# A decoder trunk's feed-forward: the pool of the V sums opened first, and two additions queued behind a reciprocal

## The chip, the cores and the metric

The kernel runs on one core of a Trainium2 chip. The metric is the device time of one execution in microseconds (us). A profile of one further execution gives a span, from its first to its last instruction, and what each engine did in it. TensorE (PE) multiplies, with its weight loads listed apart (PEld); VectorE is DVE, ScalarE is ACT, GpSimd is POOL, and SP is the engine that issues most of the transfers.

## The reference

Two residual layers on 512 tokens of 1024 features, in float32, then one more norm. Each layer adds a mixer's output and then a SwiGLU feed-forward's, each computed from the normed stream:

```
for i in range(2):
    x = x + mixer_i(rmsnorm(x, norm_mix[i]))          # 0: causal pooling, 1: dilated window attention
    h = rmsnorm(x, norm_ffn[i])
    x = x + (silu(h @ w_gate) * (h @ w_up)) @ w_down   # 2816 hidden features
return rmsnorm(x, norm_final)
```

## The kernel before

Every float32 product is made of three matmuls. A tile is split into a rounded part `hi` (a copy on ScalarE, line 137 for weights and 312 for activations) and the rest `lo` (a subtraction on VectorE, lines 138 and 313), and TensorE sums `hi*hi`, `hi*lo` and `lo*hi`.

The feed-forward works on blocks of a 2 by 2 scheme with seven products in place of eight (a Winograd form). Gate and up weights of 128 columns are cut into blocks; for the group `n`, the products 0 to 6 (`Group.product`, line 601 holds its matmuls) use a block or a sum of blocks as weights, and on the right the normed tokens: first or last 256 tokens, first or last four chunks of features, or sums of these (`t2`, `t3`, `t4`, and `T_hi[0]`, the tokens' own place rewritten). The weights of products 1, 2 and 5 are sums. They are built in a tile `vraw`, one for each group: SP loads one block (line 104), GpSimd adds a second with an accumulating transfer (line 106), and VectorE adds and subtracts other raw tiles later (line 140). `vraw` tiles come from the pool `ffv`, three of 4 KB (`V_TILES`); all other raw weights come from a ring of five `wraw`, and their splits from a ring of five pairs `whi` and `wlo`. A raw tile that a sum still needs keeps its place in the ring until line 140 has run.

One list, `queue`, holds all weight tiles in the order of their use. `weights(i)` (line 119) issues loads some places ahead and splits four places ahead; `load_sums` (line 109) issues the `vraw` loads, and does so only once the pool of the feed-forward is open. TensorE's order is the one written in the code. The order of all other engines and of the DMA queues is set by a planner that takes, at each point of its own model, the instruction that is ready and has the best priority; those within `high_priority(URGENT)` come first. [...]

Memory is handed out as a stack: each pool lies behind the pools still open, in the order of opening. With `reuse_waits="tile"` an instruction that first writes a tile waits for the last readers of the tiles that lay there. At the start of a feed-forward the pools of the mixer before it are closed, so the feed-forward's pools begin at the same address as that mixer's. In the first layer there lie, from that address on, `p_hi` (16 KB a partition), `p_lo` (16 KB), the eight tiles `bhi` and `blo` of the pool `poolb` (the second half of the output weights, 32 KB) and one of 4 KB. In the second layer there lie `pT` (41 KB), `v` (16 KB) and some small tiles with `LB`, in one pool `attn`, then the pool `merged` (8 KB), then `wob`, the eight tiles `bhi` and `blo` there. In the feed-forward (`ffn`, line 514) the pools come in the order `ffn` (`t2` to `t4`, `keep`, `ct`, 34.25 KB), `ffv` (12 KB), `ffa` (28 KB) and `ffh` (`t1r`, `t2r`, `t3r`, `b21r` and `ct_second`, 24 KB).

The join of mixer and feed-forward is `out_projection` (line 342). It makes the last product of the mixer in two halves of columns. In the second half, block by block of 128 tokens, TensorE makes the product, VectorE adds it to the stream (line 340), ScalarE squares it (line 275), and `Norm.prepare` (line 297) makes the root: `inverse_rms` (line 286) is a square root on ScalarE (line 290) and four short VectorE steps on one column (lines 291 to 294), the last of which is the reciprocal by which ScalarE then scales the rows (line 303). The rows of blocks 0 and 1 are turned (transposed on TensorE, line 309) while the next products run, those of block 2 behind the last product, and those of block 3 within the feed-forward's first stage.

That stage is "two": two groups at once, in the order `TWO`, products 0 and 3 of both first since these need only blocks 0 and 1 of the tokens. Beside them the operands of the others are made. `first_tokens` (line 639) adds `hi` and `lo` of the first 256 tokens back into whole numbers, on VectorE (line 641): `t1r` from the first four chunks of features, `b21r` from the last four. `late(b, what)` (line 645) takes blocks 2 and 3 from TensorE's bank and makes `t1r`, `t2r`, `t3r` and their splits: `t1r` in line 651, read by the last step also from `b21r` in line 662. The first addition is written ahead of the stage's loop, the second at its fifth place:

```
first_tokens(0, t1r)
for at, (g, i) in enumerate(TWO):
    ...
    if at == 4:
        first_tokens(1, b21r)
```

After "two" come groups of seven products ("quad") and the down projections.

Of the kernel before, what the change touches and what calls it, by code (L numbers as in the profile page):

```python
# [57 lines left out]
def trunk_kernel(ctx: ExitStack, tc: tile.TileContext, x_in, xT, gam, gains, consts, ident_d, w0, wT, w1, wv, w_down, out):  # L58
# [9 lines left out]
    nc = tc.nc  # L68
# [17 lines left out]
    pools = {}  # L86
    RING = 5
    V_TILES = 3
# [150 lines left out]
    def tokens_at(shift):  # L239
        return [h[:, shift : shift + NC * S].rearrange("p (c s) -> p c s", c=NC) for h in h_both]  # L240
# [17 lines left out]
    class Norm:  # L258
# [27 lines left out]
        def inverse_rms(self, b):  # L286

            v, s, r = (tmp.tile([P, 1], F32, name=name, bufs=2) for name in ("v1", "s1", "r1"))
            first, second = self.ss[:, b, 0:1], self.ss[:, b, 1:2]
            nc.scalar.activation(s, second, AF.Sqrt, bias=first)  # L290
            nc.vector.tensor_add(v, first, second)
            nc.vector.reciprocal(r, s)
            nc.vector.tensor_scalar(v, v, r, s, op0=ALU.mult, op1=ALU.add)
            nc.vector.reciprocal(r, v)
            return r

        def prepare(self, b, parts=(slice(0, D),)):
# [89 lines left out]
    with ExitStack() as pctx:  # L387
        open_pool = lambda name, bufs, **kw: pctx.enter_context(tc.tile_pool(name=name, bufs=bufs, reuse_waits="tile", **kw))
# [37 lines left out]
        norm = Norm(None, spare)  # L426
# [11 lines left out]
        v, s, r = (tmp.tile([P, 4], F32, name=name) for name in ("v4", "s4", "r4"))  # L438
# [66 lines left out]
        norm = Norm(0, px.tile([P, D], F32, name="even_rows"))  # L505
# [8 lines left out]
    def ffn(layer, norm, third, nxt):  # L514
# [8 lines left out]
        with ExitStack() as fctx:  # L523
            open_pool = lambda name, bufs, **kw: fctx.enter_context(
                tc.tile_pool(name=f"{name}{layer}", bufs=bufs, reuse_waits="tile", **kw)
            )
            fp = open_pool("ffn", 1)
            fps = open_pool("ffps", 2, space=bass.MemoryType.PSUM)
            pools["v"] = open_pool("ffv", V_TILES)
            early_u = open_pool("ffa", 2)  # L530
            h_hi, h_lo = tokens_at(SHIFT)
            block = lambda t, k, n: t[:, 4 * k : 4 * k + 4, HALVES[n]]

# [103 lines left out]
            t1r, t2r, t3r, b21r = (hn.tile([P, 4, 256], F32, name=name) for name in ("t1r", "t2r", "t3r", "b21r"))  # L637

            def first_tokens(k, to):

                nc.vector.tensor_add(to, block(h_hi, k, 0).bitcast(F32), block(h_lo, k, 0).bitcast(F32))
# [3 lines left out]
            def late(b, what):  # L645
                js = slice((b - 2) * P, (b - 1) * P)
                tps = late_banks[b]
                at = lambda t: t[:, :, js]
                parts = lambda i: (at(T_hi[i]), at(T_lo[i]))
                if what == 1:  # L650
                    nc.vector.tensor_sub(at(t1r), at(t1r), tps[0])
                    split(*parts(0), at(t1r))
                    nc.scalar.copy(at(t3r), tps[0])
                elif what == 2:
                    nc.vector.scalar_tensor_tensor(at(t2r), at(t1r), -1.0, tps[1], op0=ALU.mult, op1=ALU.subtract)
                    split(*parts(1), at(t2r))
                elif what == 3:
                    nc.vector.tensor_sub(at(t3r), tps[1], at(t3r))
                    split(*parts(2), at(t3r))
                else:  # L660
                    split(at(block(h_hi, 1, 1)), at(block(h_lo, 1, 1)), tps[1])
                    nc.vector.scalar_tensor_tensor(at(t2r), at(t2r), -1.0, at(b21r), op0=ALU.mult, op1=ALU.subtract)
                    split(*parts(3), at(t2r))
# [4 lines left out]
            def down(b):  # L668

                pairs = BLOCKS[b]  # L670

                p, r = ([fps.tile([P, 2, 256], F32, name=t).rearrange("p g c -> p (g c)") for _ in range(2)] for t in "rp")
                q = [mm.tile([P, S], F32, name="mm") for _ in range(2)]
                where = (0, 1, 2, 3, 6, 5, 4)
                target = ((0, 0, 1), (1, 1, -1), (0, 1, 1), (0, 0, 1), (1, 1, -1), (0, 1, 1), (1, 0, -1))
                for i, acc in enumerate((p, r, p, q, p, r, p)):
                    ws = [weights(js[i], held=z) for z, js in enumerate(dn[b])]
                    half, n, sign = target[i]
                    for t in range(2):
                        for c, pair in enumerate(pairs):  # L680
                            whi, wlo = (w[:, c % 2, :] for w in ws[c // 2])
                            hi, lo = (u[:, where[i], t * P : (t + 1) * P] for u in u_of[pair])
                            for k, (u, w) in enumerate(((hi, whi), (hi, wlo), (lo, whi))):
                                nc.tensor.matmul(  # L684
                                    acc[t], lhsT=u, rhs=w, start=i in (0, 1, 3) and c + k == 0,
                                    stop=c == len(pairs) - 1 and k == 2, skip_group_check=True,
                                )
                        to = x[:, 2 * n + t, COLS[half]]
                        with tc.high_priority(URGENT):
                            if sign > 0:  # L690
                                nc.vector.tensor_add(to, acc[t], to)
                            else:
                                nc.vector.tensor_sub(to, to, acc[t])

            for kind, n in FFN_ORDER[:-1]:
                if kind == "two":
                    groups = [Group(n, ct_common), Group(n + 1, ct_tile(hn, "ct_second"))]
                    first_tokens(0, t1r)
                    for at, (g, i) in enumerate(TWO):
                        if at in (0, 2):  # L700
                            b = 2 + at // 2
                            if b == 2:
                                late_banks[b] = third
                                norm.prepare(3, COLS)
                            else:
                                late_banks[b] = [r_tile(), by_four(mm.tile([P, S], F32, name="mm"))]
                                for half in range(2):
                                    norm.turn(b, half, late_banks[b][half])
                            late(b, 1)
                        if at == 4:  # L710
                            first_tokens(1, b21r)
                        if at in (4, 6, 8):
                            for b in (2, 3):
                                late(b, at // 2)
                        groups[g].product(i)
                    held.close()
                    late_u.append(open_pool("ffb", 2))
                elif kind == "quad":
                    group = Group(n, ct_common)
                    for i in range(7):  # L720
                        group.product(i)
                else:
                    down(n)


            norm = Norm(nxt, ct_common.rearrange("p m n g c -> p (m n g c)")[:, :D])
# [58 lines left out]
        return norm  # L785

    norm = ffn(0, norm, third, 1)


    with ExitStack() as actx:  # L790
# [6 lines left out]
        at = 8 * SPAN  # L797
# [4 lines left out]
        v = ap.tile([P, 4, D], F32, name="v")  # L802
# [159 lines left out]
        for t in range(8):  # L962
# [6 lines left out]
            at = 2 * t + 3  # L969
# [92 lines left out]
        for part in range(2):  # L1062
            at = VA + part * VB
# [53 lines left out]
        norm = Norm(2, mp.tile([P, D], F32, name="even_rows"))  # L1117
# [3 lines left out]
        third = out_projection(j_wo, range(NC), m_hi, m_lo, norm, SHIFT, four, lambda: [sc_tile(), sc_tile()])  # L1121

    ffn(1, norm, third, 3)


# [65 lines left out]
```

## Time and profile before

| | us |
|---|---|
| median of 3 runs | 1018.32 (1017.35 to 1019.07) |
| the profiled execution's own time | 1018.40 |
| its span | 1016.6 |
| TensorE busy in the span | 1000.0 |
| VectorE busy | 792.8 |
| ScalarE busy | 530.0 |
| GpSimd busy | 121.0 |
| mean granted TensorE clock | 0.994 of full speed |

Times in the profile count from the start of the span. A line of a timeline gives the start, the duration, the engine, the line of the code, the operation and the names of what it writes and reads; in brackets stands how long the engine had been idle before it, and the instruction or transfer that ended this. Matmuls overlap in the pipeline: one is listed with 0.28 us though the next starts 0.12 us later. So the distance between starts tells the pace, and a matmul slowed by a lower clock counts as busy all the same. `SPq` lines are issues of transfers, not their duration.

### The profile page before, as it was taken

The numbers are of one execution on the slowest core, as the hardware profiler recorded it, in microseconds if no ns is written. First come the engines' busy times: TensorE is split into PE (matmuls) and PEld (weight loads), VectorE is DVE, ScalarE is ACT, GpSimd is POOL, SyncE is SP. The second block draws the span as 40 slices with busy tenths as digits, with TensorE's granted clock in tenths as the row PEclk, the third lists the DMA queues.
The fourth block names the chain that finished last, engine by engine and source line by source line (L and its number), as shares of the span: only waits on it lengthen the run. The fifth ranks groups of instructions, "written<-read, shape, count | busy, mean of one in ns | idle before, by whom it ended". The sixth has DMA issues, their size and how long they took to land.

```text
span 1016.6 us, 16615 instructions
## 1 busy us (share of the span) xinstructions
PE 1000.0 (98%) x6582; PEld 912.5 (90%) x6582; DVE 792.8 (78%) x1134; ACT 530.0 (52%) x836; POOL 121.0 (12%) x108
## 2 busy tenths in 40 slices
PE   9999989999999999999999999999999999999997
PEld 7888879989998998989777899889998999999895
DVE  6483689898888788777988747569989888888875
ACT  5572467545654554463344444357654564455454
POOL 0000101101011100001333210100101001111000
PEclk9999989999999999999999999999999999999999
DMA  9451467759559854514311246525866955975522
GB/s 346 157 186 21 117 194 193 175 170 260 142 129 248 222 142 139 183 57 145 103 42 52 75 124 175 116 63 160 203 150 192 237 149 118 287 187 138 154 71 83
DMA packets 76349, 155.16 MB, mean 153 GB/s; under 512 B 6448, under 2 KB 6576, under 8 KB 76272
## 3 DMA queue, kind: packets, MB, share of 16 engines
q1 hardware_dynamic: 58944, 121.00, 35.5%
q0 software_dynamic: 17040, 32.84, 19.1%
q8 instruction: 51, 0.84, 0.3%
q10 hardware_dynamic: 288, 0.27, 0.1%
q14 instruction: 26, 0.21, 0.1%
HBM read 151.99 MB, written 2.10 MB: 152 GB/s over the span
## 4 chain that ended last, share of the span: by engine, by line
PE 92%; DVE 3%; DMA 2%; ACT 2%; issue 1%; POOL 0%; SPq 0%; ACTq 0%; POOLq 0%
PE p L601 24%; PE r L601 13%; PE r L684 10%; PE mm L601 6%; PE p L684 5%; PE mm L222 4%; PE mm L224 3%; PE mm L223 3%; PE mm L738 3%; PE mm L684 2%; PE mm L354 2%; PE mm L352 2%; PE mm L353 2%; DMA vraw<-w 1%; PE mm L1073 1%; PE mm L1072 1%
## 5 line engine op out<-in xcount | busy, mean ns | idle before, releaser
L138 DVE TENSOR_TENSOR wlo<-wraw,whi 128x1024 fp32r<-128x1024 f32 (+2 forms) x190 | 220.4, 1161 | 76.6 <-ACT whi L137 76.0
L137 ACT CAST whi<-wraw 128x1024 fp32r<-128x1024 f32 (+2 forms) x190 | 185.2, 978 | 173.0 <-issue 34.7
L137 ACT CAST whi<-vraw 128x1024 fp32r<-128x1024 f32 (+1 forms) x102 | 99.4, 976 | 148.0 <-DVE vraw L140 51.6
L601 PE MATMUL p<-t_hi,wlo 128*128 128x256 f32 x528 | 149.9, 284 | 0.0
L601 PE MATMUL p<-t_lo,whi 128*128 128x256 f32 x528 | 149.9, 284 | 0.0
L601 PE MATMUL p<-t_hi,whi 128*128 128x256 f32 x528 | 148.7, 282 | 0.9 <-ACT ct L616 0.9
L138 DVE TENSOR_TENSOR wlo<-vraw,whi 128x1024 fp32r<-128x1024 f32 (+1 forms) x102 | 114.9, 1127 | 19.8 <-ACT whi L137 19.3
L601 PE MATMUL r<-h_hi,whi 128*128 128x256 f32 x352 | 100.3, 285 | 3.9 <-ACT h_hi L312 3.9
L601 PE MATMUL r<-h_lo,whi 128*128 128x256 f32 x352 | 101.1, 287 | 0.1
L601 PEld LDWEIGHTS p<-t_hi,whi 128*128 128x128 f32 x528 | 100.1, 189 | 1.1 <-ACT ct L616 1.1
L601 PE MATMUL r<-h_hi,wlo 128*128 128x256 f32 x352 | 101.0, 287 | 0.0
L601 PEld LDWEIGHTS p<-t_hi,wlo 128*128 128x128 f32 x528 | 99.8, 189 | 0.0
L601 PEld LDWEIGHTS p<-t_lo,whi 128*128 128x128 f32 x528 | 99.3, 188 | 0.1
L106 POOL DMA_DIRECT2D wraw<-w x22 | 26.8, 1216 | 429.3 <-DMA wraw<-w 93.2
L140 DVE TENSOR_TENSOR vraw<-vraw,wraw 128x1024 f32<-128x1024 f32 x68 | 76.6, 1127 | 0.8
L601 PEld LDWEIGHTS r<-h_hi,whi 128*128 128x128 f32 x352 | 67.9, 193 | 4.1 <-ACT h_hi L312 4.1
L601 PEld LDWEIGHTS r<-h_lo,whi 128*128 128x128 f32 x352 | 67.4, 191 | 0.4 <-DVE h_lo L313 0.4
L601 PEld LDWEIGHTS r<-h_hi,wlo 128*128 128x128 f32 x352 | 67.6, 192 | 0.0
L222 PE MATMUL mm<-h_hi,whi 128*128 128x512 f32 (+1 forms) x176 | 65.3, 371 | 0.0
L224 PE MATMUL mm<-h_hi,wlo 128*128 128x512 f32 (+1 forms) x176 | 63.6, 361 | 0.0
L223 PE MATMUL mm<-h_lo,whi 128*128 128x512 f32 (+1 forms) x176 | 63.5, 361 | 0.0
L684 PE MATMUL r<-wlo,u_hi 128*128 128x512 f32 x144 | 56.1, 390 | 0.0
(313 smaller groups left out, 2516.4 us busy)
## 6 DMA issues: line engine op xcount, KB each, us to landing
wraw<-w SPq DMA_DIRECT2D x116, 512.0 KB, 4.9
wraw<-w_down SPq DMA_DIRECT2D x32, 512.0 KB, 3.7
wraw<-w POOLq DMA_DIRECT2D x22, 512.0 KB, 7.5
vraw<-w SPq DMA_DIRECT2D x22, 512.0 KB, 5.0
vraw<-w POOLq DMA_DIRECT2D x22, 512.0 KB, 8.9
wraw<-wT SPq DMA_DIRECT2D x16, 512.0 KB, 3.8
wraw<-w_down SPq DMA_DIRECT2D x24, 256.0 KB, 2.7
vraw<-w_down SPq DMA_DIRECT2D x6, 512.0 KB, 5.4
```

The source lines that it names most:

```text
L106: nc.gpsimd.dma_start(dst, more, accum_op=ALU.add)
L137: nc.scalar.copy(hi[:, :n], raw[:, :n])
L138: nc.vector.tensor_sub(lo[:, :n], raw[:, :n], hi[:, :n].bitcast(F32))
L140: nc.vector.tensor_add(raws[into][:, :n], raws[into][:, :n], raws[more][:, :n])
L222: nc.tensor.matmul(ps, lhsT=whi, rhs=xhi, start=first, stop=False, **kw)
L223: nc.tensor.matmul(ps, lhsT=whi, rhs=xlo, start=False, stop=False, **kw)
L224: nc.tensor.matmul(ps, lhsT=wlo, rhs=xhi, start=False, stop=last, **kw)
L352: nc.tensor.matmul(ps, lhsT=xhi, rhs=w[0][:, k, :], start=first, stop=False)
L353: nc.tensor.matmul(ps, lhsT=xhi, rhs=w[1][:, k, :], start=False, stop=False)
L601: nc.tensor.matmul(ps[:, g, :], lhsT=w[:, g, c, :], rhs=xx[:, c, :], start=i in (0, 1, 3) and g + c + k == 0, stop=c == 3 and k == 2, skip ...
L684: nc.tensor.matmul(acc[t], lhsT=u, rhs=w, start=i in (0, 1, 3) and c + k == 0, stop=c == len(pairs) - 1 and k == 2, skip_group_check=True,)
L738: nc.tensor.matmul(ps, lhsT=u, rhs=w[:, m, :], start=z + m + k == 0, stop=z == 1 and m == 1 and k == 2,)
```

## The change

Three things. The pool of the `vraw` tiles is opened ahead of the feed-forward's other pools, so that its 12 KB come first in the memory and `t2` to `ct` follow behind them; the later pools stay where they were. `inverse_rms` keeps its last instruction, the reciprocal. And both additions of `first_tokens` are written ahead of the stage's loop, with an edge that puts them behind the reciprocal kept last, that of the third block, in VectorE's order (an order of issue; they don't wait for its end). Both feed-forwards run this code.

```
@@ inverse_rms
-            nc.vector.reciprocal(r, v)
+            self.chain = nc.vector.reciprocal(r, v)
@@ ffn
+            pools["v"] = open_pool("ffv", V_TILES)
             fp = open_pool("ffn", 1)
             fps = open_pool("ffps", 2, space=bass.MemoryType.PSUM)
-            pools["v"] = open_pool("ffv", V_TILES)
             early_u = open_pool("ffa", 2)
+            third_chain = norm.chain.ins
@@ ffn, the stage "two"
-                    first_tokens(0, t1r)
+                    with tc.issue_after(third_chain):
+                        first_tokens(0, t1r)
+                        first_tokens(1, b21r)
                     for at, (g, i) in enumerate(TWO):
...
-                        if at == 4:
-                            first_tokens(1, b21r)
```

## Rows read from the trace of the kernel before

**Rows 1.** The page's first part: busy time of each engine, its share of the span and its count of instructions.

```profile
PE 1000.0 (98%) x6582; PEld 912.5 (90%) x6582; DVE 792.8 (78%) x1134; ACT 530.0 (52%) x836; POOL 121.0 (12%) x108
```

**Rows 2.** TensorE's list of waits from 105 to 170 us: what waited, for what, then total time, times and the longest, in us.

```profile
PE r L601 <- ACT h_hi L312: 3.9, 1, 3.9
PE p L601 <- ACT ct L616: 0.9, 1, 0.9
PE mm L309 <- ACT even_rows L303: 0.7, 1, 0.7
```

**Rows 3.** TensorE's timeline around the join and the "two" stage of the first feed-forward: the last matmul of the out-projection, the first product, the first `r` product, and the first `r` product of the next quad.

```profile
113.55 0.39 PE L354 MATMUL mm<-bhi,h_lo 128*128 128x512 f32 x1
...
115.46 0.36 PE L601 MATMUL p<-h_hi,whi 128*128 128x256 f32 x1
...
131.89 0.58 PE L601 MATMUL r<-h_hi,whi 128*128 128x256 f32 x1 [3.86 <-ACT h_hi L312]
...
167.72 0.28 PE L601 MATMUL r<-h_hi,whi 128*128 128x256 f32 x1
```

**Rows 4.** TensorE's timeline at the same places of the second feed-forward (last matmul of the out-projection, first product, first `r` product of the next quad).

```profile
678.44 0.40 PE L354 MATMUL mm<-bhi,h_lo 128*128 128x512 f32 x1
...
679.46 0.37 PE L601 MATMUL p<-h_hi,whi 128*128 128x256 f32 x1
...
723.18 0.28 PE L601 MATMUL r<-h_hi,whi 128*128 128x256 f32 x1
```

**Rows 5.** The table by stretches: the stretch, its length, then busy time and count of PE, PEld, DVE, ACT and POOL, the granted clock, the share of the DMA engines and GB/s. The first line is the stage "two" of the first feed-forward, the second that of the second, then two pieces of the first.

```profile
115.46:167.72 52.26, 47.31 (x371) 46.46 (x370) 42.19 (x60) 31.25 (x46) 8.48 (x7) 0.93 0.84 220
679.46:723.18 43.72, 43.72 (x372) 43.72 (x371) 42.96 (x62) 31.44 (x47) 3.61 (x3) 1.00 0.61 169
134.00:138.00 4.00, 4.00 (x22) 4.00 (x21) 4.00 (x5) 1.82 (x2) 1.21 (x1) 0.53 0.12 39
146.00:147.50 1.50, 0.56 (x5) 0.35 (x3) 0.78 (x3) 1.50 (x4) 0.00 (x0) 1.00 0.68 225
```

**Rows 6.** Issues of transfers, from the timelines of SP and GpSimd: first feed-forward (SP, then GpSimd), then SP in the second.

```profile
63.48 8.07 SPq L104 DMA_DIRECT2D wraw<-w  x5
113.97 1.39 SPq L104 DMA_DIRECT2D vraw<-w  x3
...
77.00 1.34 POOL L106 DMA_DIRECT2D wraw<-w  x1 [76.55 <-DVE h_lo L488]
118.04 1.21 POOL L106 DMA_DIRECT2D vraw<-w  x1 [39.71 <-DMA vraw<-w]
...
633.31 1.59 SPq L104 DMA_DIRECT2D vraw<-w  x3
```

**Rows 7.** The timelines of ScalarE and VectorE in the stage "two" of the first feed-forward: the split of the first V tile, and what VectorE does behind it.

```profile
127.23 1.05 ACT L137 CAST whi<-vraw 128x1024 fp32r<-128x1024 f32 x1 [6.20 <-DMA vraw<-w]
...
128.32 1.23 DVE L138 TENSOR_TENSOR wlo<-vraw,whi 128x1024 fp32r<-128x1024 f32 x1 [5.96 <-ACT whi L137]
129.46 0.68 DVE L651 TENSOR_TENSOR t1r<-t1r,r 128x512 f32<-128x512 f32 x1
```

**Rows 8.** Last readers: of `p_hi` (TensorE, first layer), of `pT` and `v` (TensorE, second layer), of `LB` (VectorE, second layer).

```profile
73.66 0.39 PE L224 MATMUL early<-p_hi,wlo 128*128 128x512 f32 x1
...
629.72 3.55 PE L1099 MATMUL mm<-pT,v 128*64 128x128 f32 x51
...
637.95 1.06 DVE L1115 TENSOR_TENSOR o<-mm,LB 128x512 f32<-128x512 f32 x1
```

**Rows 9.** From the view of all instructions on `vraw`: the time from issue to landing of its transfers.

```profile
DMA to landing us min/median/max: 3.2/6.0/12.3
```

**Rows 10.** The first V tile in the second feed-forward, from the timelines of ScalarE and VectorE.

```profile
655.35 1.04 ACT L137 CAST whi<-vraw 128x1024 fp32r<-128x1024 f32 x1
...
658.36 1.22 DVE L140 TENSOR_TENSOR vraw<-vraw,wraw 128x1024 f32<-128x1024 f32 x1
```

**Rows 11.** Timelines of VectorE and ScalarE in the first layer: the first update of `x` and the first square in the second half of the out-projection, and the copy into `keep`.

```profile
95.85 0.69 DVE L340 TENSOR_TENSOR x<-mm,x 128x512 f32<-128x512 f32 x1 [3.15 <-PE mm L354]
...
96.58 0.63 ACT L275 ACTIVATE even_rows<-x 128x512 f32<-128x512 f32 x1 [4.66 <-DVE x L340]
...
119.95 0.57 ACT L612 COPY keep<-p 128x512 f32<-128x512 f32 x1
```

**Rows 12.** VectorE's timeline around the third block's root in the first layer.

```profile
110.78 1.20 DVE L641 TENSOR_TENSOR t1r<-h_hi,h_lo 128x1024 f32<-128x1024 f32 x1
111.91 0.27 DVE L293 TENSOR_SCALAR v<-v,r,s 128x1 f32<-128x1 f32 x1
...
113.22 0.15 DVE L294 RECIPROCAL r<-v 128x1 f32<-128x1 f32 x1
113.98 0.69 DVE L340 TENSOR_TENSOR x<-mm,x 128x512 f32<-128x512 f32 x1 [0.60 <-PE mm L354]
```

**Rows 13.** VectorE's timeline around the fourth block in the second layer.

```profile
678.87 0.69 DVE L340 TENSOR_TENSOR x<-mm,x 128x512 f32<-128x512 f32 x1 [2.61 <-PE mm L354]
...
683.26 0.16 DVE L294 RECIPROCAL r<-v 128x1 f32<-128x1 f32 x1
```

**Rows 14.** Groups of the page by line, engine and operands: count, busy us and mean ns of one, and the idle time before them.

```profile
L601 PE MATMUL p<-t_hi,whi 128*128 128x256 f32 x528 | 148.7, 282 | 0.9 <-ACT ct L616 0.9
...
L601 PE MATMUL r<-h_lo,whi 128*128 128x256 f32 x352 | 101.1, 287 | 0.1
```

## The prediction

> **What bounds the kernel now.** I read the page first. TensorE is counted busy for 1000.0 of the 1016.6 us span, so a gain can only come from the stretches in which it waits or runs slowly. The next question is where those stretches are [rows 1]. The list of TensorE's waits, cut to 105 to 170 us, has three entries: 3.9 us for a ScalarE copy of `h_hi`, 0.9 us for a copy into `ct`, 0.7 us for `even_rows` [rows 2]. All three lie at the start of the first feed-forward, in or just ahead of its "two" stage. The second feed-forward runs the same code, and there TensorE has no idle time at all [rows 5]; that makes it the yardstick.
>
> The timeline gives the size. From the last matmul of the out-projection to the first product is 113.55 to 115.46, 1.91 us, in the first feed-forward [rows 3] and 678.44 to 679.46, 1.02 us, in the second [rows 4]. From that first product to the first `r` product of the next quad is 115.46 to 167.72, 52.26 us, against 679.46 to 723.18, 43.72 us, for the same instructions. [...]
>
> Now the chain behind the 3.86 us. The three loads of `vraw` are issued at 113.97, right behind the last out-projection matmul, since in the old allotment their tiles lie over the weights `bhi` that this matmul reads. GpSimd adds the second source from 118.04 on [rows 6]. The first sum can be split only at 127.23 (ScalarE idle 6.20 us for that transfer); VectorE, which works in order, stands 5.96 us at the matching `wlo`, and behind it in the queue is `t1r` of the fourth block, made at 129.46. From it comes the `h_hi` for which TensorE stands until 131.89 [rows 3, 7]. So a late weight transfer stops an operation that has nothing to do with it.
>
> **Part 1: V tiles first.** Three 4 KB tiles now take the first 12 KB of the feed-forward's memory instead of 12 KB that begin some 34 KB in. The first 16 KB there are `p_hi`, last read by the matmul at 73.66 [rows 8]. That a load waits for the tiles below it alone, and not for their whole pool, is seen in the second feed-forward: there it goes at 633.31, right behind the last matmul that reads `pT` and `v`, while `LB`, a tile of the same pool, is read until 639 [rows 6, 8]. So I expect the loads at about 74.1, 39.9 us earlier. SP's queue holds nothing between the five loads that end at 71.55 and these three, so they pass nobody; on POOL they come behind one accumulation at 77.00 [rows 6]. POOL's first V addition came 4.07 us behind SP's first load, so it is due near 78.2, and a transfer of `vraw` lands after 12.3 us at the longest [rows 6, 9]: 90.5 at worst.
>
> What takes the place of the wait? The second feed-forward shows it: there ScalarE splits the first V tile at 655.35 (1.04 us), and the addition that ends VectorE's part comes at 658.36 (1.22 us) [rows 10]. That is 23.1 us ahead of the last out-projection matmul; in the first feed-forward the same distance is about 90.5. There ScalarE is idle for 4.66 us before 96.58 and VectorE for 3.15 us before 95.85 [rows 11]; one ScalarE piece and two VectorE pieces of 1.2 us each are covered. Without that cover they would hold up the first block's root by up to 1.0 + 2.4 = 3.4 us. I take nothing. Three SP issues, 1.39 us together, and three POOL issues of 1.2 us are only moved, into empty queues.
>
> The price of the stage: the same instructions took 43.72 us with V in time, so 52.26 - 43.72 = **8.54 us**. Bounds: the single wait alone, 3.86 us, below; 8.54 above, as the twin leaves no wait to gain. I take the upper end, since all of it (wait, slow clock, the 0.94 us behind a late weight) follows from the one late transfer and the twin shows the cured state.
>
> Another reading gives less. TensorE's weight loads were busy 46.46 of the 52.26 us, 5.80 idle, against none idle in the twin [rows 5]; between 134 and 138, at a clock of 0.53, they are busy the whole time. [...]
>
> **Part 2: first tokens behind the third root.** In the first feed-forward VectorE makes `t1r` (1.20 us, at 110.78) and, in the gap between 111.91 and 113.22, `b21r` between the last steps of the third block's root, so the root comes at 113.22 and TensorE waits 0.7 us for the rows that ScalarE scales by it [rows 2, 12]. Behind the root instead: without the two additions of some 1.1 us each the root ends 2.2 us sooner, near 111.0 to 111.2, three times the wait, so the transposes follow the last matmul at once. The additions then take about 111.3 to 113.6, and the next operation, the update of `x` at 113.98, waits for TensorE anyway (0.60 us idle before it). If they ran over, that update would slip by what is left. With the second feed-forward's 1.02 us for this join the gain is 1.91 - 1.02 = **0.89 us** (at least the 0.7 of the wait).
>
> In the second feed-forward the third root is already clear of them. There `t1r` lies over a `wob` tile that is read until the last matmul, so it stays behind the update of `x` at 678.87; `b21r`, now asked for earlier, can fall into VectorE's idle 2.61 us before that update or come right after `t1r`, ahead of the fourth block's root, which ends at 683.26 [rows 13]. Between a gain of nothing (TensorE doesn't wait here) and a loss of the 1.1 us of one addition I take nothing: no product waits here now, and its work has to be done before the same products in either order.
>
> **Other moves.** `t2` to `t4`, `keep` and `ct` go up by 12 KB; in the first feed-forward part of them now lies over `bhi`, free when the last matmul at 113.55 ends, and the first of these to be written, `keep`, is due at 119.95 [rows 3, 11]. 6 us cover it; without them that copy, and the sum that reads it, would slip by what is left. Matmuls take 282 ns on a `t` tile and 287 on `h`, at quite other addresses [rows 14]: I take nothing. The spread of these means, 5 ns, on the 1584 matmuls of `t` bounds it at 7.9 us either way, less than the 9.43 us gained below.
>
> **Sum.** The profiled execution took 1018.40 us (span 1016.6 and 1.8 around it), 0.08 above the median of the runs, 1018.32. 1018.40 - 8.54 - 0.89 = 1008.97, so 1009.0.
>
> **Rivals.**
> - *The wait shrinks but the clock still falls.* V is in time, yet another late piece (the fourth block's `t1r` behind a split, a weight waiting for a tile) stops TensorE for longer than 0.94 us. For: VectorE is nearly full in this stage, 42.96 of 43.72 us even in the twin [rows 5]. Against: the twin never waits. What the half clock took beyond the idle time is 8.54 - 5.80 = 2.74 us; if that stays, 1009.0 + 2.7 = 1011.7. [...] Chance 0.12.
> - *V does not move*, because the load is released by something later than `p_hi`, or sits elsewhere in SP's order. Then only part 2 counts: 1018.40 - 0.89 = 1017.5. Against it, the tile-wise release of [rows 6, 8]. Chance 0.06.
> - *Slower: the early split blocks ScalarE in the out-projection.* The split at 90.5 waits for the GpSimd addition, and squares, roots and turns of all four blocks are queued behind it. ScalarE's next own work is due at 96.58 [rows 11], so it costs nothing until the sum lands after 95.5; from there on each us late is at most a us of TensorE, and past 95.5 + 9.4 = 104.9 the kernel is slower than before. At 110 it would be 1009.0 + 14.5 + 2.7 for the clock = 1026. The longest landing, 12.3 us [rows 9], speaks against it. Chance 0.04.
>
> **How the numbers follow.** The forecast has 0.78. Runs lay from 1017.35 to 1019.07, so about 0.9 either way; with up to 1.1 us lost in the second feed-forward and a few tenths from other orders on VectorE, the forecast's own span is 1007.6 to 1011.0. Reaching over the first rival and its scatter, 1011.7 + 0.9, I give 1007.6 to 1012.6. The bound for a difference is 0.2%, 2.04 us: about what a measurement of this kernel can tell from none. Forecast and first rival are faster, 0.90; the second is within the bound, 0.06; the third slower, 0.04.
>
> **What would show it.** Right: SP's first three `vraw` loads near 74, the first V split near 90 to 92, no TensorE wait for `h_hi`, a clock of 1.00 in the stage, the stage 43.7 to 44 us, the join about 1.0 us, both `L641` behind the third root. Wrong: `vraw` still issued near 114, or a new entry over 1 us in the list of TensorE's waits between 85 and 165 or between 675 and 725, or a `L601` mean on `t` tiles above 288 ns.

## The result

The changed kernel took 1008.98 us (median of 4 runs, 1007.82 to 1010.05) against 1018.10 (1017.35 to 1019.07) for the kernel before: a ratio of 0.9908, 95% interval [0.9893, 0.9923]. The prediction was 1009.0, in a range of 1007.6 to 1012.6.

Over all its 14 runs the changed kernel fell into two groups: 6 runs at 1007.82 to 1008.14 and 8 at 1009.69 to 1010.49. All three profiled ones are of the upper group and show where the 2 us are: in the first products, which start 0.425 us apart until about 10 us and 0.23 us apart from there on (last section), far from what was changed.

**The profile after.** The changed kernel's page, first part and the clock row of the second: to be read against [rows 1]. TensorE's busy time fell by 2.7 us, the span (1008.2) by 8.4; every slice now shows a nine for the clock.

```profile
PE 997.3 (99%) x6582; PEld 910.3 (90%) x6582; DVE 792.9 (79%) x1134; ACT 530.3 (53%) x836; POOL 121.0 (12%) x108
...
PEclk9999999999999999999999999999999999999999
```

The four largest of TensorE's waits over the whole span of the changed kernel: nothing is over 1.1 us. None of the three entries of [rows 2] is left.

```profile
PE mm L256 <- DVE odd_rows L250: 1.1, 1, 1.1
PE tp L921 <- ACT pT L926: 0.9, 1, 0.9
PE sc L852 <- DVE e L860: 0.6, 1, 0.6
PE early L222 <- ACT whi L137: 0.6, 1, 0.6
```

The changed kernel's table by stretches: a stretch of its beginning, then the two "two" stages, to be read against [rows 5].

```profile
7.00:9.70 2.70, 2.70 (x7) 2.06 (x7) 1.59 (x3) 2.06 (x3) 0.00 (x0) 1.00 1.02 400
116.61:160.30 43.69, 43.69 (x372) 43.69 (x371) 41.12 (x60) 31.59 (x47) 3.63 (x3) 1.00 0.61 170
671.57:715.28 43.71, 43.71 (x372) 43.71 (x371) 43.06 (x62) 31.21 (x47) 3.61 (x3) 1.00 0.61 169
```

The first feed-forward's stage now takes as long as the second's, at a clock of 1.00. The timelines of the changed kernel show why: SP, GpSimd, ScalarE, VectorE and TensorE in turn, answering [rows 3, 6, 7, 12].

```profile
65.52 8.04 SPq L104 DMA_DIRECT2D wraw<-w  x5
76.12 1.39 SPq L104 DMA_DIRECT2D vraw<-w  x3
96.79 0.37 SPq L104 DMA_DIRECT2D wraw<-w  x1
...
81.33 2.66 POOL L106 DMA_DIRECT2D vraw<-w  x2
88.55 1.23 POOL L106 DMA_DIRECT2D vraw<-w  x1 [4.56 <-issue]
...
92.50 1.04 ACT L137 CAST whi<-vraw 128x1024 fp32r<-128x1024 f32 x1
...
95.51 1.22 DVE L140 TENSOR_TENSOR vraw<-vraw,wraw 128x1024 f32<-128x1024 f32 x1
...
113.24 0.17 DVE L294 RECIPROCAL r<-v 128x1 f32<-128x1 f32 x1
113.32 1.21 DVE L642 TENSOR_TENSOR t1r<-h_hi,h_lo 128x1024 f32<-128x1024 f32 x1
114.44 1.22 DVE L642 TENSOR_TENSOR b21r<-h_hi,h_lo 128x1024 f32<-128x1024 f32 x1
116.02 0.69 DVE L340 TENSOR_TENSOR x<-mm,x 128x512 f32<-128x512 f32 x1 [0.35 <-PE mm L354]
...
75.70 0.39 PE L224 MATMUL early<-p_hi,wlo 128*128 128x512 f32 x1
...
115.58 0.40 PE L354 MATMUL mm<-bhi,h_lo 128*128 128x512 f32 x1
115.82 1.04 PE L309 MATMUL mm<-ident,even_rows 128*128 128x128 f32 x8
116.61 0.37 PE L602 MATMUL p<-h_hi,whi 128*128 128x256 f32 x1
...
160.30 0.28 PE L602 MATMUL r<-h_hi,whi 128*128 128x256 f32 x1
```

V's loads go at 76.12 instead of 113.97, behind the last matmul that reads `p_hi` (75.70); the first split, at 92.50, waits for nothing. Both first-token sums stand behind the third root, and the transposes follow the last matmul without a gap.

This execution runs 2.03 us behind the kernel before from 10 us on, up to the end of the out-projection. In the stretch 7.00 to 9.70 TensorE did 7 products; the reordered kernel of the experiments (e5) did 14 in the same stretch. (The clock of 1.00 in the first line of the table above is not a measurement; the last section says why.) Measured from the last out-projection matmul to the next quad's first `r` product, which leaves the beginning out, the kernel before took 167.72 - 113.55 = 54.17 us [rows 3] and the changed one 160.30 - 115.58 = 44.72: **9.45 us less**. The span's 8.4 is 9.45 + 0.94 - 2.03; 0.83 of the 0.94 is a pace of TensorE, told in the last section.

### The profile page after: what moved, and what is told of

Its sections match the earlier page's. It is cut to its first block, busy times and chain, and to the rows that moved or that the text cites. A ratio compares the mean times of both kernels' runs of the same rounds, so it can differ in the third digit from the quotient of the medians.

```text
span 1008.2 us, 16621 instructions
## 1 busy us (share of the span) xinstructions
PE 997.3 (99%) x6582; PEld 910.3 (90%) x6582; DVE 792.9 (79%) x1134; ACT 530.3 (53%) x836; POOL 121.0 (12%) x108
## 4 chain that ended last, share of the span: by engine, by line
PE 94%; DVE 3%; ACT 1%; issue 1%; DMA 0%; POOL 0%; SPq 0%; ACTq 0%; POOLq 0%
PE p L602 25%; PE r L602 13%; PE r L685 10%; PE mm L602 6%; PE p L685 5%; PE mm L222 4%; PE mm L224 3%; PE mm L223 3%; PE mm L739 3%; PE mm L685 2%; PE mm L354 2%; PE mm L352 2%; PE mm L353 2%; PE early L222 1%; PE early L223 1%; PE early L224 1%
## 5 line engine op out<-in xcount | busy, mean ns | idle before, releaser
L685 PE MATMUL r<-whi,u_lo 128*128 128x512 f32 x144 | 56.1, 390 | 0.0
```

What stands on the lines that cost most here:

```text
L685: nc.tensor.matmul(acc[t], lhsT=u, rhs=w, start=i in (0, 1, 3) and c + k == 0, stop=c == len(pairs) - 1 and k == 2, skip_group_check=True,)
```

## The experiments

All are run on one core beside the kernel before, which had medians of 1017.8 to 1018.7 us in these runs. "Held" and "late" speak of the first V tiles of the first feed-forward.

**e1: the V pool alone.** The memory order as changed, the first tokens where they were:

```
+ pools["v"] = open_pool("ffv", V_TILES)
  fp = open_pool("ffn", 1)
  ...
- pools["v"] = open_pool("ffv", V_TILES)
```

> The V pool first, the first tokens' additions left where they were in the kernel before. My theory (the late V transfer costs the stage 8.5 us, the additions within the third root cost the join 0.7 to 0.9 us, and the two add up): V loads near 74 to 76, the stage 43.7 us, the 0.7 us wait for even_rows still there, so about 9.4 - 0.9 = 8.5 us faster than before, some 0.9 us slower than the full change: 1009.6 to 1010.0. Rival (the additions' place is what frees VectorE's queue, V's place alone does little): under 4 us faster, TensorE still waits for h_hi.

Measured: 1009.39 us, ratio 0.9911 [0.9890, 0.9931]. Its loads go at 74.13, the first split at 90.52; the only wait of TensorE left between 100 and 170 is the one for the third block's rows:

```profile
PE mm L309 <- ACT even_rows L303: 0.7, 1, 0.7
```

The stage takes 43.73 us (115.51 to 159.24) at a granted clock of 1.00. So the memory order alone takes away the long wait and the half clock (0.50 from 131.0 to 137.7 us in the kernel before).

**e2: the first tokens alone.** V where it was:

```
- first_tokens(0, t1r)
+ with tc.issue_after(third_chain):
+     first_tokens(0, t1r)
+     first_tokens(1, b21r)
```

> The additions behind the third root, the V pool where it was. The sum in the prediction adds its two parts, so by it 0.9 us faster: 1017.2. Rival (the parts are not independent): the V loads go with the last out-projection matmul, whose time doesn't move, so the wait in the stage ends at V's landing as before and grows by what the join saves: the 0.7 us wait goes from the join, but the whole is not faster by it. In the planned order t1r of the fourth block now stands ahead of the V split on VectorE, so the wait could end up to 1.7 us earlier than in the kernel before: 1016.4 to 1018.1 by this rival. In either case V loads right behind the last matmul and a slow clock behind the wait.

Measured: 1019.96 us, ratio 1.0015 [1.0002, 1.0028]: no gain, rather a loss. Both expectations missed. The list of TensorE's waits in this kernel, 100 to 170 us, has lost the 0.7 for `even_rows` and won another:

```profile
PE p L602 <- ACT t_hi L312: 4.2, 1, 4.2
PE r L602 <- ACT h_hi L312: 1.4, 1, 1.4
PE r L602 <- DVE h_lo L313: 1.0, 1, 1.0
PE p L602 <- DVE t_lo L313: 0.3, 1, 0.3
```

The timelines of SP and ScalarE in e2 say what released them:

```profile
113.86 1.39 SPq L104 DMA_DIRECT2D vraw<-w  x3
...
130.91 3.83 SPq L104 DMA_DIRECT2D wraw<-w  x2
...
126.81 1.04 ACT L137 CAST whi<-vraw 128x1024 fp32r<-128x1024 f32 x1 [5.78 <-DMA vraw<-w]
...
142.59 1.04 ACT L137 CAST whi<-wraw 128x1024 fp32r<-128x1024 f32 x1 [5.76 <-DMA wraw<-w]
...
146.39 0.63 ACT L312 CAST t_hi<-t3r 128x512 fp32r<-128x512 f32 x1
```

The join took 1.02 us (113.44 to 114.46) in place of 1.91, as intended, but the products then only meet the late tiles sooner. `t1r` now stands ahead of the split that waits, so the first wait is shorter; the next tiles of W1 are loaded only at 130.91 (in the changed kernel the first of them goes at 96.79), and the split of one of them stops ScalarE ahead of a `t_hi`: TensorE waits 4.25 us before 147.07. The granted clock is 0.50 from 131 to 133 and 0.75 from 146 to 150, so the half clock is met twice.

**e4: the queue order alone.** In the kernel before, `late(b, 1)`, which makes `t1r` of the third and fourth block, gets a higher priority, so that the fourth block's comes ahead of the V split on VectorE:

```
- late(b, 1)
+ with tc.high_priority(URGENT):
+     late(b, 1)
```

> The kernel before, with the residual of the fourth block's first tokens (t1r of the second quad) made at high priority, so that VectorE has it ahead of the splits of V that wait for their transfer. V's tiles stay where they were. Theory (the late transfer of V is the root, and holds W1's ring as well): the wait for h_hi is split up or moves to the next t_hi, and the time is 1017 to 1020. Rival (the root is the order on VectorE, in which t1r stands behind a split that waits): the 3.86 us go, 1014 to 1015, with no half-clock stretch after 130 us.

Measured: 1018.72 us, ratio 1.0006 [0.9994, 1.0017]: the theory's case. `t1r` is done at 123, yet `h_hi` is still copied on ScalarE behind the V splits, at 130.17. From the timelines of VectorE, ScalarE and TensorE:

```profile
122.31 0.68 DVE L651 TENSOR_TENSOR t1r<-t1r,r 128x512 f32<-128x512 f32 x1
...
130.17 0.61 ACT L312 CAST h_hi<-t1r 128x512 fp32r<-128x512 f32 x1
...
130.84 0.58 PE L601 MATMUL r<-h_hi,whi 128*128 128x256 f32 x1 [2.84 <-ACT h_hi L312]
```

TensorE waits 2.84 us for it, then 2.51 us before 146.81 behind a W1 tile. Moving `t1r` ahead of the late tile on one engine left its copy behind the same tile on the other.

**e5: V in another early place.** The changed kernel, with `t2` and `t3` first and V's tiles behind them, over `p_lo` of the first layer's mixer (the causal pooling; the expectation calls it the attention):

```
+ t2, t3 = (...)                          # in a pool of their own, first
  pools["v"] = open_pool("ffv", V_TILES)
  ...
+ t4 = ...
```

> The changed kernel with another order in the feed-forward's memory: the second and third blocks' t pieces first, then V's tiles, then the fourth block's pieces and ct. V's tiles then lie over other memory that the attention leaves early. Theory (any place that is free before the out-projection does): 1008 to 1010, V's loads issued before 95 us, no wait for h_hi. Rival (only the place at the very start is early enough; this one is freed by the attention's last readers, late): 1012 to 1018. Beside that: if the pace of the 256-column products (118.7 or 120.0 ns) goes with V's address, it changes here against the changed kernel by up to 0.5 us for each feed-forward; if not, it is the same.

Measured: 1008.84 us, ratio 0.9909 [0.9890, 0.9928], the same as the change. Loads at 73.96, right behind the last matmul that reads `p_lo` (73.54, 0.39 us long), and from the last out-projection matmul (113.66) to the first product (114.68) 1.02 us. Its table by stretches: the beginning and the stage "two".

```profile
7.00:9.70 2.70, 2.70 (x14) 2.21 (x13) 0.69 (x1) 1.46 (x3) 0.00 (x0) 1.00 1.03 407
114.68:158.36 43.68, 43.68 (x371) 43.68 (x370) 41.11 (x60) 31.57 (x47) 3.63 (x3) 1.00 0.62 170
```

So it need not be the start of the memory: a second place that the mixer leaves early does as well.

**e3: the layout as changed, the transfer held.** One column of a block of the residual `x` is copied into each of the first three raw tiles before its load, so the load waits for that block (here the fourth, index 3; the other three alike with 2, 1 and 0):

```
+ if item["kind"] == "v" and len(loaded["v"]) < V_TILES:
+     nc.vector.tensor_copy(raw[:, 0:1], x[:, 3, S : S + 1])
  nc.sync.dma_start(dst, item["src"][0])
```

> The changed kernel with the V tiles in their new place, but the first three loads held back: each tile is first written (one column, from the stream's block 3, by VectorE), so its load can't go before the last update of x in the out-projection, about 1 us behind its last matmul. If the time of the transfer is what counts, the stage has its wait and slow clock again, and the whole takes 1017.5 to 1019.5. If the memory layout or VectorE's order is what counts, it stays at 1009 to 1010.

> As the run with block 3, but held by block 2 of the stream: the loads go some 6 us earlier, about 5 us ahead of the last matmul. From issue to split the first V tile took 13.3 us in the kernel before, and its product is due some 13.4 us behind the last matmul, so by the time theory it is ready 3 us or more ahead of it and the wait does not come back: 1009 to 1010.5. If the loads have to be as early as in the full change (splits under the out-projection's cover), TensorE waits again for 1 us or more in the stage, and it takes 1011 or longer.

> The changed kernel, with each of the first V transfers held until VectorE has copied one column of the stream's second block (index 1) of the feed-forward's residual into its raw tile. The layout stays as changed; only the time of the loads moves, to about 104 us, between the 76 of the changed kernel and the 111 of the hold by block 2. Theory A (what costs is V's arrival after the place that its split has in the queues of ScalarE and VectorE, and those places are now about 116 to 119 us): the first V tile arrives 12 to 13 us after its issue, at 116 to 118, so nearly nothing is lost: 1008.5 to 1011. Rival B (any load behind the out-projection's work costs, since it also holds up the ring of W1's tiles): 1012 to 1017, with a half-clock stretch after 116 us.

> The changed kernel, with each of the first V transfers held until VectorE has copied one column of the stream's first block (index 0) of the feed-forward's residual into its raw tile: the loads start near 98 to 99 us, some 23 us later than in the changed kernel and 6 earlier than in the hold by block 1. Theory (a load costs only if its tile is not there when the in-order queues of ScalarE and VectorE reach its split; 12 us after the issue is about 110 to 111): if the split now stands after that, nothing is lost, 1008.5 to 1010, with no wait of TensorE for more than 1 us between 95 and 140 us. Rival (the loss grows evenly with the time of the loads, by the line through the three holds measured so far, 0.46 us for each us): about 1011 to 1012.

Measured: 1018.95 us, 1.0011 [0.9993, 1.0028], held by the fourth block (loads at 115.32); 1016.77, 0.9986 [0.9971, 1.0001], by the third (111.04); 1013.97, 0.9952 [0.9935, 0.9970], by the second (104.54); 1017.35, 0.9992 [0.9981, 1.0004], by the first (96.80). The fourth came as expected: with the new layout but about the old load time, TensorE waits 2.8 us for `h_hi` again, the clock falls again (0.994 on average over the span, as in the kernel before, against 0.998 in the changed one), and the gain is gone. The others all missed, and not in one direction: the load at 96.80 costs more than the one at 104.54. So neither "early enough is free" nor an even loss for each us holds. What differs is the work behind the split. In the kernel held by the first block, the timelines of SP, ScalarE, VectorE and TensorE:

```profile
96.80 1.39 SPq L106 DMA_DIRECT2D vraw<-w  x3
...
108.87 1.04 ACT L139 CAST whi<-vraw 128x1024 fp32r<-128x1024 f32 x1 [5.27 <-DMA vraw<-w]
112.60 1.15 ACT L305 ACTIVATE odd_rows<-odd_rows,r 128x1024 f32<-128x1024 f32 x1 [2.68 <-DVE r L296]
...
109.94 1.23 DVE L140 TENSOR_TENSOR wlo<-vraw,whi 128x1024 fp32r<-128x1024 f32 x1 [5.43 <-ACT whi L139]
111.09 0.27 DVE L295 TENSOR_SCALAR v<-v,r,s 128x1 f32<-128x1 f32 x1
...
113.80 1.97 PE L311 MATMUL early<-ident,odd_rows 128*128 128x128 f32 x8 [6.22 <-ACT odd_rows L305]
```

The planned order puts the split into the middle of the second block's root: `v` is multiplied, 6 us late, behind `wlo`. TensorE stands 6.22 us at that block's transposes, with matmuls of the out-projection queued behind them; the feed-forward's stage, 43.68 us, loses nothing. Held by the second block, ScalarE stands 3.83 us for the tile and TensorE 3.9; by the third, 5.90 and 5.4; both times TensorE waits for `odd_rows` of the fourth block, within the stage. In all these, and in the kernel before, ScalarE is at the split 6.0 to 7.9 us after the loads' issue (split time less its wait), and the tile is there after 11.7 to 13.3. That the planner reckons with a shorter transfer than the chip's is inferred from these distances; its model is not on record.

In these rows nothing passes a split that waits: ScalarE runs nothing in the 5.27 us ahead of 108.87, and VectorE nothing in the 5.43 us ahead of 109.94, with the root's next step behind that, at 111.09.

**e8: the same late load, the split moved.** The kernel held by the first block, with the split of the first V tile told to come behind the third root:

```
+ if first:
+     anchored.enter_context(tc.issue_after(loaded["anchor"]))
  nc.scalar.copy(hi[:, :n], raw[:, :n])
  ...
```

> The hold by block 0 as before (V's first three loads start at 96.8 us), with the split of the first V tile now put behind the third block's root, about 111 us, when its data have been there since 108.9. Nothing else differs by hand. Theory (the loss comes from the place of the split in the in-order queues of ScalarE and VectorE, which the planned order put 5 us ahead of the data's arrival): the 6.2 us wait of TensorE goes and the time falls back to 1008 to 1010. Rival (the time of the load itself costs, through the transfers queued behind it or the ring of W1's tiles): 1013 to 1018, with waits of TensorE behind 120 us in place of the one at 107.

Measured: 1013.68 us, ratio 0.9959 [0.9945, 0.9972]: between the two. Its timelines show that half of the edit took: VectorE's half of the split moved behind the root and the first tokens, ScalarE's half stayed ahead of the second block's `odd_rows`.

```profile
96.87 1.39 SPq L106 DMA_DIRECT2D vraw<-w  x3
...
107.50 1.04 ACT L143 CAST whi<-vraw 128x1024 fp32r<-128x1024 f32 x1 [3.83 <-DMA vraw<-w]
108.45 1.14 ACT L309 ACTIVATE odd_rows<-odd_rows,r 128x1024 f32<-128x1024 f32 x1
...
115.72 1.22 DVE L144 TENSOR_TENSOR wlo<-vraw,whi 128x1024 fp32r<-128x1024 f32 x1
...
109.64 1.09 PE L315 MATMUL early<-ident,odd_rows 128*128 128x128 f32 x8 [1.99 <-ACT odd_rows L309]
```

And its table by stretches behind that wait, with two products from within it:

```profile
111.84 0.63 PE L359 MATMUL mm<-blo,h_hi 128*128 128x512 f32 x1
112.27 0.63 PE L360 MATMUL mm<-bhi,h_lo 128*128 128x512 f32 x1
...
110.00:115.00 5.00, 5.00 (x20) 4.06 (x19) 4.52 (x10) 3.02 (x6) 0.00 (x0) 0.66 0.46 84
```

TensorE's wait shrank from 6.22 to 1.99 us with the load at the same time. The tile was there 1.4 us sooner (ScalarE splits at 107.50 against 108.87), which can explain 1.4 us of this; the rest, most of the wait, came from the place of VectorE's half in its queue. The 1.99 us left stand behind ScalarE's half, which waits 3.83 us for the tile. Matmul by matmul against e5, this kernel loses 2.1 us by 109.64, another 1.7 by the end of the out-projection (the half clock) and 0.2 more up to the next quad (3.98 us there). With V's load at 96.87, TensorE's list of waits has no entry in the feed-forward's stage. The expectation of 1008 to 1010 was not reached; what a split wholly behind the root would give wasn't run.

**e6 and e7: the change again, and beside the V pool alone on one chip.**

> The changed kernel itself, once more, to stand beside the V pool's move alone on the same footing. Theory (the V move is worth about 9.0 us and the early first tokens another 0.8 once V is out of the way): 1008.0 to 1009.3, and in the trace, lined up stage by stage, 0.8 us less than with the V pool moved alone from the third root on. Rival (the tokens give nothing: something else takes up the 0.8): 1009.4, no less than the V pool's move alone.

> The V pool's move alone, on the same chip as the next run: 1008.8 to 1009.8, and the 0.7 us wait for even_rows still there.

> The changed kernel on the same chip as the V pool's move alone. Theory (the early tokens are worth 0.7 to 0.9 us once V is early): the better runs at 1008.0 to 1008.2, 0.7 to 0.9 under the better runs of the V pool's move alone; runs whose first products go at half pace are up to 2 us above that. Rival (the tokens give nothing even then): no difference between the better runs of the two.

Measured: e6 1008.91 us, ratio 0.9907 [0.9889, 0.9925]. In e7 the V pool alone had 1009.05 (1008.89 to 1011.49), 0.9919 [0.9903, 0.9935], and the whole change 1009.81 (1008.12 to 1010.49), 0.9915 [0.9900, 0.9930]. The better runs differ as the theory says, 1008.12 and 1008.14 against 1008.89 to 1009.08; in the two profiles the join takes 1.91 us with the V pool alone and 1.03 with the whole change. But four of the six runs of the whole change lie 1.6 to 2.4 us above its better ones, and two of the six of the V pool alone 2.2 to 2.6 above its own, so by the medians the early tokens bring nothing that can be told from zero.

## Why the prediction was right

**Part 1: right in place, size and mechanism.** It said 52.26 to 43.72, 8.54 us; measured 52.26 to 43.69, 8.57. That it is the time of the loads that counts is shown from both sides: e1 and e5 gain with early loads in two places, and the changed layout with late loads (e3, fourth block) gains nothing. The twin in the second feed-forward was the right yardstick: e1, e5 and the change all come to its length. The loads were forecast for 74.1 (74.13 in e1, 73.96 in e5, 76.12 in the change, which began 2 us late), the tile for 90.5 at worst. That the first split began at 90.52 in e1 is luck: it waited for nothing there and began behind ScalarE's own work. One link of the chain was told too narrowly: `t1r` behind the V split on VectorE. In e4 `t1r` was early (122.31) and `h_hi` still came late (130.17), since ScalarE stood 5.94 us for the same tile. The idle time of the weight loads alone would have put this stage's gain at 5.80; the stage's length says 8.57. That measure leaves out the half clock, here 2.8 us.

**Part 2: right in its term, wrong as an item on its own.** It said 1.91 to 1.02 for the join, 0.89 us; in the change it is 116.61 - 115.58 = 1.03, so 0.88. In the second feed-forward nothing was to change: 670.54 to 671.57, 1.03 against 1.02 [rows 4], although `b21r` there did come between the steps of the fourth root. So the sum, 8.54 + 0.89 = 9.43, stands against a measured 9.45.

**The total is closer than it had a right to be.** The median 1008.98 lies midway between a run of each group (1008.11 and 1009.85), and none of the 14 runs is within 0.6 us of 1009.0: the better ones, near 1008.0, lie 1.0 below it, the others 0.7 to 1.5 above. The sum knew nothing of two things that the profiled execution shows, 0.94 us gained, 0.83 of it from TensorE's pace, and 2.03 lost at the beginning. So the two terms are confirmed by the trace, and the agreement to 0.02 us is luck.

**What failed.** The rival that V does not move read "then only part 2 counts", 1017.5 us. e2 is that case, and it took 1019.96. The step behind it, that the two parts add, is wrong: an earlier join is worth something only if the late tile doesn't end the wait anyway, and a late V also holds back the tiles of W1 that are loaded behind its split.

The slower rival was the right danger in the wrong form. It let an early split cost nothing until its sum came after 95.5, a limit read from ScalarE's next work at a fixed order. The order is not fixed: in the kernels with held loads ScalarE reached the split 6.0 to 7.9 us after the issue, at four different places of the out-projection and the stage. In the changed kernel 16.4 us pass between the issue (76.12) and the split (92.50), more than the 13.3 us that the tile took at most where ScalarE waited for it; why the planned order leaves more there is not shown. The held loads had less than half of that and lost 5 to 10 us: by the first block all in the out-projection, as that rival had it, by the others in the stage.

The first rival, that the clock would still fall behind another wait, did not occur in the changed kernel. But it also fell behind a wait shorter than the 3.86 us: the 1.99 us of e8 were followed by a granted clock of 0.66 from 110 to 115, while around the 0.94 us of the kernel before it was 1.00 [rows 5]. From what length on a wait brings it is not shown.

## What to carry to other kernels

When an engine stands for a DMA and other work is queued behind that, look at what memory the destination lies over: here its last reader set the load time (issue at 76.12 behind a read at 75.70), and the cure may be the order in which tiles are allotted. Then compare the distance from issue to first use in the planned order with the time that the tile takes in the trace: where the order reckons with too short a transfer, whatever stands behind the use is blocked (here TensorE stood 6.22, 3.9 and 5.4 us for loads at 96.80, 104.54 and 111.04), and the loss depends on that work and not only on how late the load is. If the kernel has a twin of the stage in which the wait is absent, its length prices the whole cure, the slow clock included (here 43.72 us, and 43.69 was reached); and two savings around one late transfer are not to be added: here one of them alone gained nothing. Where a profile prints a clock, ask whether a record of it covers the stretch, and check it by the pace.

## What the runs showed of the hardware

- **The changed kernel's first products ran at the pace of the lower clock, and the printed 1.00 hides it.** In its profiled execution the first 128x512 products started 0.425 us apart until 10.15, then 0.23:

```profile
7.17 0.63 PE L222 MATMUL early<-whi,h_hi 128*128 128x512 f32 x1
7.60 0.63 PE L223 MATMUL early<-wlo,h_hi 128*128 128x512 f32 x1
...
10.15 0.39 PE L223 MATMUL early<-wlo,h_hi 128*128 128x512 f32 x1
10.38 0.40 PE L224 MATMUL early<-whi,h_lo 128*128 128x512 f32 x1
```

  The table prints a granted clock of 1.00 for 7.00 to 9.70, but the trace has no clock record there: its records begin at 10.13 us in this execution, at 4.65 in the kernel before's. The stretch without a record is printed as 1.00. The pace changes where the first record begins. In the profiles of e6 and e7's whole change it changes at 9.62 and 9.47; like this one (7), they did few products from 7.00 to 9.70 (8 each), the eleven other profiles 13 or 14, all with a printed 1.00. And in e8, in the stretch with a granted clock of 0.66 (110 to 115, by estimate 3.4 us of it at the 0.50 that the kernel before's records show), products of the same size also start 0.425 us apart and are listed with 0.63 us. So the first products ran at the pace that e8 shows under the lower clock, in this execution until the first record. What TensorE did ahead of it was alike: sixteen transposes from 1.09 us, then the first product between 5.0 and 5.5, in this kernel as in the kernel before. Why the faster pace comes later in these executions of this kernel, and whether the change has a part in it, is open; that all eight times of the upper group have this cause fits the three profiles but is not shown for the rest, nor for the two higher times of the V pool alone.
- **Two paces of the 256-column products.** TensorE ran these 118.7 or 120.0 ns apart on average, both at a granted clock of 1.00. The kernel before fell to 120.0 at 165 us of the first feed-forward and at 720 of the second, the changed one only after the third quad. From the end of the stage "two" to the first 512-column product that is 37.44 us to 37.02 in the first feed-forward and 37.44 to 37.03 in the second: 0.83 of the 0.94 us between the two profiles. It does not follow the time of V's loads: e3 held by the first block, with loads at 96.80, kept 118.7 through the three quads of both feed-forwards, while e5, with loads at 73.96, fell at 710 in the second. Whether V's place has a part in it is open, as is the cause, so those 0.94 us are not counted as the change's.
- **From issue to use of a V tile.** From the issue of three V loads to the first split, which needs a load and the GpSimd sum on it, 10.6 us (e8) to 13.3 us (kernel before) passed in every kernel in which ScalarE waited for it.
